# Hybrid decoder block on one core: attention scores in two PSUM tiles of 512 keys in place of one of 1024, the bias of the exponentials on ScalarE, and the sums without copies

## The chip, the core and the metric

The kernel runs on one core of one Trainium2 chip. The metric is the device time of one execution in microseconds (us). Before the change three runs gave 2529.47, 2530.45 and 2536.47 us, median 2530.45 us. One execution was profiled; it took 2535.77 us, with a span of 2534.0 us from its first to its last instruction.

Engines are named as the profile names them: PE (TensorE, matmuls), PEld (its weight loads), DVE (VectorE), ACT (ScalarE), POOL (GpSimd), SP (SyncE, which issues most DMAs). Each engine works through its own queue in order; what stands behind a waiting instruction waits too.

## The reference

One decoder sub-layer on x of 2048 tokens by 1024 channels: RMS norm, one input projection into seven parts, a gated linear recurrence (RG-LRU) in one branch, differential attention in the other, gates, an output projection and a second RMS norm. The change touches the attention:

```python
def diff_attention(q, k, v, lam):          # q, k: (B, S, 8 heads, 2 components, 64); v: (B, S, 8, 128)
    scale = HEAD_DIM ** -0.5
    outs = []
    for qb in range(S // Q_BLOCK):         # 16 blocks of 128 queries
        q0 = qb * Q_BLOCK; q1 = q0 + Q_BLOCK
        s = jnp.einsum('bqhcd,bkhcd->bhcqk', q[:, q0:q1], k[:, :q1]).astype(jnp.float32) * scale
        mask = (q0 + jnp.arange(Q_BLOCK))[:, None] >= jnp.arange(q1)[None, :]
        s = jnp.where(mask, s, -jnp.inf)
        p = jax.nn.softmax(s, axis=-1)
        w = p[:, :, 0] - lam * p[:, :, 1]
        outs.append(jnp.einsum('bhqk,bkhe->bqhe', w, v[:, :q1]))
    return jnp.concatenate(outs, axis=1)
```

Each head has two score matrices (components). Each gets a causal softmax of its own, the second is subtracted with the weight lam, and the difference multiplies v.

## The kernel before

The program has three stages. The first normalises x and runs the recurrence branch. The second, attention, also computes the projections q, k, v, za and gm as "fills" between its pieces of work. The third merges the branches. Every float32 matmul is done as three float16 matmuls (high by high, high by low, low by high).

Attention works in 128 units: 8 heads (h) of 16 query blocks (t), in this order. A unit has t+1 key blocks of 128 keys. They are cut into pieces of at most 8 blocks (1024 keys): one piece for t below 8, two from t = 8 on. The steps of a unit are:

- `a_scores(u, pi)` for one piece: the matmuls of line L804 write a PSUM tile `sc` of 128 queries x 2 components x 1024 keys, that is four PSUM banks. The pool `ps_s` has one such buffer, so the first matmul of a piece waits until DVE has read the whole piece before it. For each group of 512 keys there are six matmuls, three for each component; the components lie on rows 0 to 63 and 64 to 127 of the array. Then DVE copies each component into an SBUF tile `e` and takes the row maximum into a column of `mx` on the way (L819); the last 128 keys get the mask added (L823).
- `a_exp(u)`: DVE reduces the columns of `mx` to `rm` (L834) and makes the bias `nb` = -scale * maximum + a small term `lsp` (L837, a tensor_scalar with two per-partition scalars). ACT takes the exponentials of each component and piece in place, with their row sums into `sm` (L843).
- `a_comb(u)`, one unit later: DVE adds the sums of two pieces (L854), takes the reciprocal (L858), copies the sum of component 0 into `s0` for later (L859), makes the factor `rs` (L860) and combines the two components (L866). ACT rounds the result to float16 (L868), POOL makes the rest (L869), and SP issues DMA transposes into `pt` (L872).
- `a_pv(u)`, three units later (LAG = 3): matmuls of `pt` with V into the PSUM tile `o` (L889). After every fourth unit `a_norm` normalises four blocks and sends them to DRAM.

A fill is a group of matmuls into the PSUM tile `mm`: 24 of 512 columns for k, q or gm (L192), 48 of 256 columns for v and za (L696), followed by evictions on ACT and DVE. Which fill comes where is set by two things: the loop at the end of the stage counts how many fills are due per unit (the string ORD gives the order of steps in a unit), and the framework that builds the program then orders each engine's queue with a cost model of its own, by what it takes to be ready, so rows of different steps interleave. [...]

Of the kernel before, what the change touches and what calls it, by code (L numbers as in the profile page):

```python
# [9 lines left out]
F32 = mybir.dt.float32  # L10
# [4 lines left out]
AF = mybir.ActivationFunctionType  # L15
# [9 lines left out]
CH = 512  # L25
# [23 lines left out]
def kernel(  # L49
# [44 lines left out]
    with ExitStack():  # L94
# [485 lines left out]
        with ExitStack() as ax:  # L580
# [11 lines left out]
            ps_s = ax.enter_context(tc.tile_pool(name="ps_s", bufs=1, space=PSUM))  # L592
# [192 lines left out]
            def a_scores(u, pi):  # L785

                h, t = u.h, u.t
                if pi == 0:
                    u.n = 1 if t == 0 else (2 if t <= 8 else 3)
                    u.mx = t4.tile([128, 2, 3], F32, tag="mx", name="mx")  # L790
                    u.e = {}
# [3 lines left out]
                pss = ps_s.tile([128, 2, 1024], F32, tag="sc", name="sc")  # L795
                q0 = (t % 4) * 128
                Q = Qt[h, t // 4]
                for x in range(0, nb, 4):
                    m = min(4, nb - x) * 128
                    K = Kt[h, (b0 + x) // 4]  # L800
                    for i, (a, b) in enumerate(((0, 0), (0, 1), (1, 0))):
                        for ci in range(2):
                            r = slice(64 * ci, 64 * ci + 64)
                            nc.tensor.matmul(pss[:, ci, x * 128:x * 128 + m], Q[r, a, q0:q0 + 128], K[r, b, 0:m],  # L804
                                             start=(i == 0), stop=(i == 2))
                last = b0 + nb == t + 1
                m = (nb - 1 if last else nb) * 128
                for ci in range(2):
                    ps = pss[:, ci]
# [7 lines left out]
                    col = pi  # L817
                    if m:
                        nc.vector.tensor_scalar(out=ev[:, 0:m], in0=ps[:, 0:m], scalar1=1.0, scalar2=None,  # L819
                                                op0=ALU.mult, op1=ALU.max, accum_out=u.mx[:, ci, col:col + 1])  # L820
                        col += 1
                    if last:
                        nc.vector.tensor_tensor_reduce(out=ev[:, m:m + 128], in0=ps[:, m:m + 128], in1=mask,  # L823
                                                       op0=ALU.add, op1=ALU.max, scale=1.0, scalar=-3e38,
                                                       accum_out=u.mx[:, ci, col:col + 1])
# [20 lines left out]
            def a_comb(u):  # L846
                h, t = u.h, u.t
                pcs = pieces(t)
                if t % 4 == 0:
                    s0_t[h, t // 4] = t4.tile([128, 4], F32, tag="s0", name="s0")  # L850
# [350 lines left out]
```

## Time and profile before

| | before |
|---|---|
| median of 3 runs | 2530.45 us (2529.47 to 2536.47) |
| profiled execution, time / span | 2535.77 us / 2534.0 us |
| attention stage in that span (first score matmul to last product with V) | about 480 to 1986 us |
| mean granted TensorE clock | 0.976 |
| PE busy, share of the span | 2338.9 us, 92% |
| DVE busy | 1549.1 us, 61% |
| ACT busy | 1224.8 us, 48% |
| POOL busy | 672.9 us, 27% |

The profile's page lists, for each group of instructions, the busy time, the mean length of one in ns, and the idle time of the engine just before them with what ended it. A window row gives, for a stretch of the span, the busy time of PE, PEld, DVE, ACT and POOL (the number of instructions in brackets), then the granted PE clock, the share of DMA and GB/s. A row of the timeline gives start, length, engine, line, operation, output and inputs, count, and in square brackets the engine's idle time before it. "PE sc L804 <- DVE e L819" in the view of waits reads: PE, at the matmuls of line 804 into `sc`, waited for the instruction of line 819 on DVE.

### The profile page before, as it was taken

The page shows a single profiled execution, that of the slowest core. Times are in us where ns is not written, and L with a number is a line of the kernel's source. Part 1 is how long each engine was busy: PE and PEld are TensorE (multiplying, and loading weights), DVE is VectorE, ACT ScalarE, POOL GpSimd, SP SyncE. Part 2 cuts the span into 40 slices and gives each one's busy share as a digit, 9 for nine tenths or more (in the row PEclk, how much of TensorE's full clock was granted, in tenths as well). Part 3 has the DMA queues.
Part 4 walks back from the last instruction along what each step waited for, and adds up shares of the span by engine and source line. Part 5 has one row for each costly group of instructions (what it writes and reads, how often), then busy time and mean ns, then how long its engine had stood idle before and what let it go on. Part 6 is the DMA issues. An engine that isn't in the chain of part 4 may idle for free. (4 is left out here: it accounts for less than half of the span.)

```text
span 2534.0 us, 42086 instructions
## 1 busy us (share of the span) xinstructions
PE 2338.9 (92%) x15880; PEld 1303.1 (51%) x15880; DVE 1549.1 (61%) x4316; ACT 1224.8 (48%) x2156; POOL 672.9 (27%) x415
## 2 busy tenths in 40 slices
PE   5699999898997999998998998898999799999998
PEld 5344444455654555654654654555655344444443
DVE  7877767667667567568568466467567244634323
ACT  5455545556556456556556455456455244312211
POOL 2343334222213213222123122222223133322211
PEclk9899999999999999999999999999999899999999
DMA  9511111134434435436335335334334844743202
GB/s 242 103 42 45 47 42 34 50 81 96 92 69 99 95 62 113 81 59 125 73 64 127 56 77 109 70 74 114 68 73 103 261 156 135 227 163 110 90 17 100
DMA packets 511627, 243.58 MB, mean 96 GB/s; under 512 B 365384, under 2 KB 488320, under 8 KB 511424
## 3 DMA queue, kind: packets, MB, share of 16 engines
q1 hardware_dynamic: 508448, 231.56, 38.0%
q0 software_dynamic: 2816, 9.08, 1.2%
q8 instruction: 124, 2.03, 0.3%
q14 instruction: 79, 0.65, 0.1%
q10 hardware_dynamic: 160, 0.27, 0.0%
HBM read 110.79 MB, written 41.94 MB: 60 GB/s over the span
## 5 line engine op out<-in xcount | busy, mean ns | idle before, releaser
L192 PEld LDWEIGHTS <-w 128*128 128x128 f16 x5040 | 473.6, 100 | 618.7 <-issue 132.2
L192 PE MATMUL mm<-uT,w 128*128 128x512 f16 x3072 | 707.2, 388 | 25.3 <-ACT gm L713 16.4
L869 POOL TENSOR_TENSOR e<-e,e 128x1024 f16<-128x1024 f32 (+2 forms) x192 | 310.9, 1633 | 859.4 <-ACT e L868 421.5
L843 ACT ACTIVATE e<-e,nb,sc_h 128x1024 f32<-128x1024 f32 (+7 forms) x384 | 376.3, 981 | 209.3 <-DVE nb L837 142.8
L192 PE MATMUL ps<-uT,w 128*128 128x512 f16 (+1 forms) x1968 | 351.0, 343 | 31.6 <-ACT xr L318 20.7
L696 PE MATMUL mm<-wva,uT 128*128 128x256 f16 x3072 | 350.2, 274 | 3.8 <-DVE wva L178 2.5
L1086 PE MATMUL psb<-yt,w 128*128 128x512 f16 x1536 | 336.2, 382 | 4.9 <-DMA yt<-ya_d 3.4
L819 DVE TENSOR_SCALAR_CACHE_REDUCE e<-sc 128x1024 f32<-128x1024 f32 (+7 forms) x352 | 304.8, 879 | 37.1 <-PE sc L804 32.0
L696 PEld LDWEIGHTS <-uT 128*128 128x128 f16 x3072 | 297.0, 98 | 56.8 <-issue 19.9
L804 PE MATMUL sc<-K,Q 64*128 64x512 f16 (+3 forms) x1920 | 214.6, 351 | 49.7 <-DVE e L819 34.5
L1086 PEld LDWEIGHTS <-w 128*128 128x128 f16 x1536 | 149.7, 98 | 187.7 <-issue 8.2
L889 PE MATMUL o<-V,pt 128*128 128x128 f16 x3264 | 215.9, 220 | 28.3 <-DMA pt<-e 28.2
L889 PEld LDWEIGHTS <-pt 128*128 128x128 f16 x3264 | 189.4, 98 | 73.5 <-DMA pt<-e 34.8
L868 ACT ACTIVATE e<-e 128x1024 f16<-128x1024 f32 (+2 forms) x192 | 150.1, 802 | 138.3 <-DVE e L866 135.4
L866 DVE SCALAR_TENSOR_TENSOR e<-e,rs,e 128x1024 f32<-128x1024 f32 (+2 forms) x192 | 194.7, 1041 | 2.6
L804 PEld LDWEIGHTS <-Q 64*128 64x128 f16 x1920 | 78.1, 95 | 153.8 <-DVE e L819 40.1
L1117 PE MATMUL psf<-wo,m 128*128 128x512 f16 x720 | 155.7, 379 | 0.0
L156 ACT ACTIVATE jk<-wst 128x1024 bf16<-128x1024 f32 x80 | 84.3, 1053 | 140.4 <-DMA wst<-in_w_in_dram 103.2
L1117 PEld LDWEIGHTS <-m 128*128 128x128 f16 x768 | 75.1, 98 | 90.6
L1090 DVE SCALAR_TENSOR_TENSOR t<-gt,psb 128x512 f32<-128x512 f32 x64 | 43.9, 686 | 120.7 <-PE psb L1086 100.1
L916 POOL TENSOR_TENSOR y<-y,y 128x512 f16<-128x512 f32 x32 | 43.4, 1357 | 261.2 <-ACT y L913 238.7
L854 DVE TENSOR_TENSOR s<-sm 128x2 f32<-128x2 f32 x64 | 11.7, 182 | 155.9 <-ACT e L843 155.8
(249 smaller groups left out, 2398.0 us busy)
## 6 DMA issues: line engine op xcount, KB each, us to landing
wst<-in_w_in_dram SPq DMA_DIRECT2D x64, 512.0 KB, 4.4
xt<-in_x_dram SPq DMA_DIRECT2D x32, 512.0 KB, 4.5
gm_d<-gm SPq DMA_DIRECT2D x64, 256.0 KB, 2.6
gt<-gm_d SPq DMA_DIRECT2D x32, 512.0 KB, 3.8
ya_d<-yT SPq DMA_DIRECT2D x64, 128.0 KB, 2.0
wst<-in_w_br_rnn_dram SPq DMA_DIRECT2D x16, 512.0 KB, 4.5
wst<-in_w_br_attn_dram SPq DMA_DIRECT2D x16, 512.0 KB, 4.5
wost<-in_w_out_dram SPq DMA_DIRECT2D x16, 512.0 KB, 3.6
```

What stands on the lines that cost most here:

```text
L156: nc.scalar.activation(jk, w.st, AF.Square, accum_out=ss)
L192: nc.tensor.matmul(ps, w.t[:, a, k, :], uT[:, b, k, c0:c0 + n], start=(i == 0), stop=(i == 3 * KD - 1))
L696: nc.tensor.matmul(ps[:, j, :], uT[:, a, k, s0:s0 + 128], wt[:, b, k].rearrange("p t f -> p (t f)"), start=(i == 0), stop=(i == 3 * KD - 1))
L804: nc.tensor.matmul(pss[:, ci, x * 128:x * 128 + m], Q[r, a, q0:q0 + 128], K[r, b, 0:m], start=(i == 0), stop=(i == 2))
L819: nc.vector.tensor_scalar(out=ev[:, 0:m], in0=ps[:, 0:m], scalar1=1.0, scalar2=None, op0=ALU.mult, op1=ALU.max, accum_out=u.mx[:, ci, col: ...
L843: nc.scalar.activation(ev[:, 0:nb * 128], ev[:, 0:nb * 128], AF.Exp, bias=nb_[:, ci:ci + 1], scale=sc_h[h], accum_out=u.sm[:, pi, ci:ci + 1])
L866: nc.vector.scalar_tensor_tensor(out=e0[:, 0:m], in0=e1v[:, 0:m], scalar=rs, in1=e0[:, 0:m], op0=ALU.mult, op1=ALU.add)
L868: nc.scalar.activation(e1[:, 0, 0:m], e0[:, 0:m], AF.Copy)
L869: nc.gpsimd.tensor_tensor(out=e1[:, 1, 0:m], in0=e0[:, 0:m], in1=e1[:, 0, 0:m], op=ALU.subtract)
L889: nc.tensor.matmul(o, pt[:, a, kb % 8, :], V[:, kb % 4, b, :], start=(kb == 0 and i == 0), stop=(kb == n - 1 and i == 2))
L1086: nc.tensor.matmul(ps, w.t[:, p, k, :], y_t[b][:, q, k, sl], start=(i == 0), stop=(i == 3 * KD - 1))
L1117: nc.tensor.matmul(pn[n], m16[:, a, j, ms], wo[:, b, j, ns], start=(j == 0 and a == 0 and b == 0), stop=(j == KD - 1 and a == 1))
```

## The change

The score tile becomes 128 x 2 x 512 (two banks), and the pool has two of them; a piece of 1024 keys uses both, one after the other. DVE copies each tile of 512 keys out by itself, each with its own column of `mx` (up to five columns instead of three). The `e` tiles in SBUF, the exponentials and all that follows keep their sizes of up to 1024 keys. The bias `nb` is made on ACT by an activation with scale and bias given per partition. The sums of the exponentials of a unit with one piece are accumulated directly into the tile `s0`, and the sum over two pieces is written there; the copy of L859 is gone.

```diff
-            ps_s = ax.enter_context(tc.tile_pool(name="ps_s", bufs=1, space=PSUM))
+            ps_s = ax.enter_context(tc.tile_pool(name="ps_s", bufs=2, space=PSUM))
...
                 if pi == 0:
-                    u.n = 1 if t == 0 else (2 if t <= 8 else 3)
-                    u.mx = t4.tile([128, 2, 3], F32, tag="mx", name="mx")
+                    u.n = t // 4 + (2 if t % 4 else 1)
+                    u.mx = t4.tile([128, 2, 5], F32, tag="mx", name="mx")
...
-                pss = ps_s.tile([128, 2, 1024], F32, tag="sc", name="sc")
...
-                for x in range(0, nb, 4):
-                    m = min(4, nb - x) * 128
-                    K = Kt[h, (b0 + x) // 4]
-                    for i, (a, b) in enumerate(((0, 0), (0, 1), (1, 0))):
-                        for ci in range(2):
-                            r = slice(64 * ci, 64 * ci + 64)
-                            nc.tensor.matmul(pss[:, ci, x * 128:x * 128 + m], Q[r, a, q0:q0 + 128], K[r, b, 0:m],
-                                             start=(i == 0), stop=(i == 2))
-                last = b0 + nb == t + 1
-                m = (nb - 1 if last else nb) * 128
...
-                    if m:
-                        nc.vector.tensor_scalar(out=ev[:, 0:m], in0=ps[:, 0:m], scalar1=1.0, scalar2=None,
-                                                op0=ALU.mult, op1=ALU.max, accum_out=u.mx[:, ci, col:col + 1])
-                        col += 1
-                    if last:
-                        nc.vector.tensor_tensor_reduce(out=ev[:, m:m + 128], in0=ps[:, m:m + 128], in1=mask,
-                                                       op0=ALU.add, op1=ALU.max, scale=1.0, scalar=-3e38,
-                                                       accum_out=u.mx[:, ci, col:col + 1])
+                for x in range(0, nb, 4):
+                    w = min(4, nb - x)
+                    K = Kt[h, (b0 + x) // 4]
+                    ps = ps_s.tile([128, 2, CH], F32, tag="sc", name="sc")
+                    for i, (a, b) in enumerate(((0, 0), (0, 1), (1, 0))):
+                        for ci in range(2):
+                            r = slice(64 * ci, 64 * ci + 64)
+                            nc.tensor.matmul(ps[:, ci, 0:w * 128], Q[r, a, q0:q0 + 128], K[r, b, 0:w * 128],
+                                             start=(i == 0), stop=(i == 2))
+                    last = b0 + x + w == t + 1
+                    m = (w - 1 if last else w) * 128
+                    col = (b0 + x) // 4
+                    for ci in range(2):
+                        ev = u.e[ci, pi][1][:, x * 128:(x + w) * 128]
+                        if m:
+                            nc.vector.tensor_scalar(out=ev[:, 0:m], in0=ps[:, ci, 0:m], scalar1=1.0, scalar2=None,
+                                                    op0=ALU.mult, op1=ALU.max, accum_out=u.mx[:, ci, col:col + 1])
+                        if last:
+                            k = col + 1 if m else col
+                            nc.vector.tensor_tensor_reduce(out=ev[:, m:m + 128], in0=ps[:, ci, m:m + 128], in1=mask,
+                                                           op0=ALU.add, op1=ALU.max, scale=1.0, scalar=-3e38,
+                                                           accum_out=u.mx[:, ci, k:k + 1])
...
-                nc.vector.tensor_scalar(out=nb_, in0=rm, scalar1=nsc_h[h], scalar2=lsp, op0=ALU.mult, op1=ALU.add)
-                u.sm = t4.tile([128, 2, 2], F32, tag="sm", name="sm")
+                nc.scalar.activation(nb_, rm, AF.Identity, scale=nsc_h[h], bias=lsp)
+                if t % 4 == 0:
+                    s0_t[h, t // 4] = t4.tile([128, 4, 2], F32, tag="s0", name="s0")
+                u.s = s0_t[h, t // 4][:, t % 4, :]
+                if t >= 8:
+                    u.sm = t4.tile([128, 2, 2], F32, tag="sm", name="sm")
...
-                                             scale=sc_h[h], accum_out=u.sm[:, pi, ci:ci + 1])
+                                             scale=sc_h[h], accum_out=(u.sm[:, pi, ci:ci + 1] if t >= 8 else u.s[:, ci:ci + 1]))
...
-                nc.vector.tensor_copy(out=s0, in_=s[:, 0:1])
```

The queues are ordered anew, since the framework sees other tiles. Two places show what the prediction speaks of.

The first is DVE at the unit h = 1, t = 14 (after its first tile is scored). Before, with `e_8166` and `e_8168` the SBUF tiles of its first piece, `y` the output of `a_norm`, `wva` the weights of v and za, `e_7914`, `e_8003` the tiles of the unit before:

```order
L910 SCALAR_TENSOR_TENSOR y<-o,rv,G 128x128 x4
L854 TENSOR_TENSOR s<-sm 128x2
L858 RECIPROCAL rs<-s 128x1
L859 COPY s_7971<-s 128x1
L860 SCALAR_TENSOR_TENSOR rs<-s,nlam,rs 128x1
L866 SCALAR_TENSOR_TENSOR e_7914<-e_7916,rs,e_7914 128x1024
L866 SCALAR_TENSOR_TENSOR e_8003<-e_8006,rs,e_8003 128x768
L178 SCALAR_TENSOR_TENSOR wva<-wst,w_sg_aza,wva 128x8x128
L819 TENSOR_SCALAR e_8166,mx<-sc 128x1024
L819 TENSOR_SCALAR e_8168,mx<-sc 128x1024
```

And now, with `e_8171` and `e_8172` the same two tiles (lines of the changed kernel: L820 is the copy out, L856 the sum, L865 the combination):

```order
L178 SCALAR_TENSOR_TENSOR wva<-wst,w_sg_aza,wva 128x8x128
L164 TENSOR_SCALAR w_tot<-tot 128x1
L105 TENSOR_SCALAR pb<-w_tot 128x1
L107 TENSOR_SCALAR w_sg_agm<-pb 128x1
L820 TENSOR_SCALAR e_8171,mx<-sc 128x512
L115 TENSOR_SCALAR w_iv_agm<-w_sg_agm 128x1
L820 TENSOR_SCALAR e_8172,mx<-sc 128x512
L171 SCALAR_TENSOR_TENSOR w_cz<-w_iv_agm,cu 128x1
L820 TENSOR_SCALAR e_8171,mx<-sc 128x512
L820 TENSOR_SCALAR e_8172,mx<-sc 128x512
L856 TENSOR_TENSOR s_7879<-sm 128x2
```

Two copies out have become four of half the size, and they stand ahead of the sums and the combinations of the unit before instead of behind them; the copy L859 is gone.

The second is PE at the first piece of h = 4, t = 15, where its first 512 keys end (`sc` with a number is one PSUM tile, `pt` and `o` belong to the product with V). Before:

```order
L804 LDWEIGHTS Q_14548
L804 MATMUL sc_15266<-K_12966,Q_14548 128x512
L804 LDWEIGHTS Q_14548
L804 MATMUL sc_15266<-K_13612,Q_14548 128x512
L804 LDWEIGHTS Q_14548
```

And now:

```order
L812 LDWEIGHTS Q_14598
L812 MATMUL sc_15326<-K_13015,Q_14598 128x512
L888 LDWEIGHTS pt_14983
L888 MATMUL o_15425<-V_13139,pt_14983 128x128
L812 LDWEIGHTS Q_14598
L812 MATMUL sc_15335<-K_13653,Q_14598 128x512
```

The two halves of a piece go to different tiles, and other matmuls may stand between them. Over the whole queue the score matmuls form 194 unbroken runs before and 245 now; their number, 1920, and that of all other matmuls is the same.

On ACT each unit's exponentials now have an activation of 128 x 2 for `nb` ahead of them in the queue (128 more instructions).

More of the change, by code (lines that the diff above doesn't have):

```diff
@@ L794, in a_scores @@
                 b0, nb = pieces(t)[pi]
-                pss = ps_s.tile([128, 2, 1024], F32, tag="sc", name="sc")
                 q0 = (t % 4) * 128
                 Q = Qt[h, t // 4]
-                for x in range(0, nb, 4):
-                    m = min(4, nb - x) * 128
-                    K = Kt[h, (b0 + x) // 4]
-                    for i, (a, b) in enumerate(((0, 0), (0, 1), (1, 0))):
-                        for ci in range(2):
-                            r = slice(64 * ci, 64 * ci + 64)
-                            nc.tensor.matmul(pss[:, ci, x * 128:x * 128 + m], Q[r, a, q0:q0 + 128], K[r, b, 0:m],
-                                             start=(i == 0), stop=(i == 2))
-                last = b0 + nb == t + 1
-                m = (nb - 1 if last else nb) * 128
                 for ci in range(2):
-                    ps = pss[:, ci]
                     if ci == 0:
@@ L816, in a_scores @@
                     u.e[ci, pi] = (e, ev)
-                    col = pi
-                    if m:
-                        nc.vector.tensor_scalar(out=ev[:, 0:m], in0=ps[:, 0:m], scalar1=1.0, scalar2=None,
-                                                op0=ALU.mult, op1=ALU.max, accum_out=u.mx[:, ci, col:col + 1])
-                        col += 1
-                    if last:
-                        nc.vector.tensor_tensor_reduce(out=ev[:, m:m + 128], in0=ps[:, m:m + 128], in1=mask,
-                                                       op0=ALU.add, op1=ALU.max, scale=1.0, scalar=-3e38,
-                                                       accum_out=u.mx[:, ci, col:col + 1])
+                for x in range(0, nb, 4):
[20 more added lines that the diff above has]
+                                                           accum_out=u.mx[:, ci, k:k + 1])
             s0_t = {}
@@ L848, in a_comb @@
                 pcs = pieces(t)
-                if t % 4 == 0:
-                    s0_t[h, t // 4] = t4.tile([128, 4], F32, tag="s0", name="s0")
-                s0 = s0_t[h, t // 4][:, t % 4:t % 4 + 1]
+                s = u.s
                 if len(pcs) == 2:
-                    s = t4.tile([128, 2], F32, tag="s", name="s")
                     nc.vector.tensor_tensor(out=s, in0=u.sm[:, 0], in1=u.sm[:, 1], op=ALU.add)
-                else:
-                    s = u.sm[:, 0]
                 rs = t4.tile([128, 1], F32, tag="rs", name="rs")
                 nc.vector.reciprocal(out=rs, in_=s[:, 1:2])
-                nc.vector.tensor_copy(out=s0, in_=s[:, 0:1])
                 nc.vector.scalar_tensor_tensor(out=rs, in0=s[:, 0:1], scalar=nlam, in1=rs, op0=ALU.mult, op1=ALU.mult)
@@ L902, in a_norm @@
                 v = t4.tile([128, 4], F32, tag="v", name="v")
-                nc.vector.tensor_scalar(out=v, in0=s0, scalar1=kap_h[h], scalar2=None, op0=ALU.mult)
+                nc.vector.tensor_scalar(out=v, in0=s0[:, :, 0], scalar1=kap_h[h], scalar2=None, op0=ALU.mult)
                 nc.vector.tensor_tensor(out=v, in0=v, in1=v, op=ALU.mult)
```

## The prediction

> **What bounds the kernel now.** I read the page first, then the attention stage alone, then what PE waits for there.
>
> ```profile
> PE 2338.9 (92%) x15880; PEld 1303.1 (51%) x15880; DVE 1549.1 (61%) x4316; ACT 1224.8 (48%) x2156; POOL 672.9 (27%) x415
> 480.00:1990.00 1510.00, 1399.04 (x11206) 844.96 (x11205) 981.82 (x3232) 833.77 (x1695) 360.30 (x228) 0.98 0.41 88
> ```
>
> The first row is the page's, the second the window of the attention stage. PE is busy for 1399.04 of 1510.00 us there and idle for 111; DVE is busy for 65% and ACT for 55%. PE is the bound, and since the change leaves its matmuls as they are, what it can win lies in those 111 us. The view of waits tells what ended them:
>
> ```profile
> PE sc L804 <- DVE e L819: 34.5, 19, 10.0
> PE o L889 <- DMA pt<-e: 28.2, 22, 3.0
> PE sc L804 <- DVE mx L823: 7.9, 12, 1.1
> PE sc L804 <- DVE rs_a L124: 2.2, 1, 2.2
> PE sc L804 <- DVE w_tot L164: 2.0, 1, 2.0
> PE sc L804 <- DVE w_iv_agm L115: 1.6, 1, 1.6
> ```
>
> The columns are the total in us, the number of waits and the longest. 48 us are score matmuls that wait for the one score tile to be read out. The next row, 28.2 us, is products with V that wait for the transposes. The change works on the first kind.
>
> **The score tile in halves: the waits.** PE may write the first 512 keys of a piece as soon as the first 512 keys of the piece before are read, instead of all 1024. What that is worth is the time between the two:
>
> ```profile
> 1007.62 1.22 DVE L819 TENSOR_SCALAR_CACHE_REDUCE e<-sc 128x1024 f32<-128x1024 f32 x1
> 1008.76 0.08 DVE L819 DVE_READ_ACCUMULATOR e<-sc 128x1 f32 x1
> 1347.90 0.68 DVE L819 TENSOR_SCALAR_CACHE_REDUCE e<-sc 128x512 f32<-128x512 f32 x1
> 1348.51 0.08 DVE L819 DVE_READ_ACCUMULATOR e<-sc 128x1 f32 x1
> ```
>
> These timeline rows give what an eviction takes until DVE's next instruction can start: 1.14 us for 1024 keys (1008.76 - 1007.62), 0.61 us for 512 (1348.51 - 1347.90). A whole piece of two components takes 2.28 us, its first half 1.22 us, so a wait can shrink by 1.06 us, not more, as long as DVE begins as late as before. Of the 34.5 us, one wait has 10.0; the other 18 have 24.5, a mean of 1.36. Their ceiling is 18 x 1.06 = 19 us; since several must be shorter than 1.06 us I take 15. The twelve of the mask row are at most 1.1 us each, so all 7.9 us go. The three single ones give 3 x 1.06 = 3.2 us. Together 26.1 us; the bounds are 0 and 48.
>
> The 10 us wait is a case of its own:
>
> ```profile
> 813.03 1.12 DVE L910 SCALAR_TENSOR_TENSOR y<-o,rv,G 128x128 f32<-128x128 f32 x4 [3.52 <-DMA gm_d<-gm]
> 814.08 0.15 DVE L854 TENSOR_TENSOR s<-sm 128x2 f32<-128x2 f32 x1
> 817.75 3.14 DVE L178 SCALAR_TENSOR_TENSOR wva<-wst,w_sg_aza,wva 128x1024 f16<-128x1024 f32 x1
> 820.80 1.21 DVE L819 TENSOR_SCALAR_CACHE_REDUCE e<-sc 128x1024 f32<-128x1024 f32 x1
> 823.23 2.42 PE L804 MATMUL sc<-K,Q 64*128 64x512 f16 x12 [9.99 <-DVE e L819]
> 825.63 6.45 PE L192 MATMUL mm<-uT,w 128*128 128x512 f16 x24
> 833.41 5.35 PE L192 MATMUL mm<-uT,w 128*128 128x512 f16 x24
> 813.20:835.00 21.80, 11.81 (x58) 4.60 (x58) 14.42 (x33) 11.57 (x19) 6.36 (x3) 0.77 0.50 122
> ```
>
> The evictions at 820.80 stood behind the sums and combinations (814.08 to 817.75, 3.67 us). This is the first place that the change's order shows, and there they come ahead of these. So this wait loses 3.67 + 1.06 = 4.7 us; nothing to 10 are its bounds. Behind it PE ran slow: the same 24 matmuls took 6.45 us instead of 5.35, the score matmuls 2.42 us, and the granted clock was 0.77 in that window. That is some 2 us: 1.1 from the 24 and about 1 from the scores. Whether PE still runs slow behind a wait of 5 us is open, so I take 1 of the 2. [...]
>
> **The score tile in halves: what it costs PE.** A run of score matmuls has a price of its own where it begins or ends:
>
> ```profile
> 962.89 0.82 PE L804 MATMUL sc<-K,Q 64*128 64x512 f16 x6 [0.58 <-DVE s L859]
> 963.64 5.41 PE L696 MATMUL mm<-wva,uT 128*128 128x256 f16 x48
> 968.99 1.47 PE L804 MATMUL sc<-K,Q 64*128 64x512 f16 x12
> 970.39 0.18 PE L162 MATMUL tot<-w_s,ones 128*128 128x1 bf16 x1
> ```
>
> Six matmuls take 0.75 us to the next start (963.64 - 962.89), twelve take 1.40 (970.39 - 968.99), and twice six would be 1.50: 0.10 us for a split. The order has 245 runs in place of 194, so 51 x 0.10 = 5.1 us are added to PE, and nothing hides them.
>
> **What it costs and frees on DVE.** The forms of L819 and the instructions that go:
>
> ```profile
> L819 DVE TENSOR_SCALAR_CACHE_REDUCE e<-sc 128x1024 f32<-128x1024 f32 x128 | 151.4, 1219 | 14.5 <-PE sc L804 12.0 <-DMA pt<-e 2.4
> L819 DVE TENSOR_SCALAR_CACHE_REDUCE e<-sc 128x896 f32<-128x896 f32 x32 | 34.7, 1086 | 3.5 <-PE sc L804 2.4 <-POOL e L869 1.1
> L819 DVE TENSOR_SCALAR_CACHE_REDUCE e<-sc 128x768 f32<-128x768 f32 x32 | 30.4, 951 | 2.0 <-PE sc L804 2.0
> L819 DVE TENSOR_SCALAR_CACHE_REDUCE e<-sc 128x640 f32<-128x640 f32 x32 | 26.2, 818 | 3.2 <-PE sc L804 3.2
> L837 DVE TENSOR_SCALAR nb<-rm,nsc_h,lsp 128x2 f32<-128x2 f32 x120 | 49.0, 409 | 2.5
> L859 DVE COPY s<-sm 128x1 f32<-128x1 f32 x64 | 9.7, 152 | 41.8 <-ACT e L843 41.8
> L859 DVE COPY s<-s 128x1 f32<-128x1 f32 x64 | 8.6, 135 | 0.0
> ```
>
> The four forms above 512 keys, 128 + 3 x 32 = 224 instructions, are split in two. Each split costs 2 x 0.61 - 1.14 = 0.08 us, 17.9 us in all. The 120 biases (49.0 us) and the 128 copies (18.3 us) go. DVE is some 49 us freer in the stage. I count nothing for that: DVE is idle for 528 us of it, and what matters is when an eviction starts, which is priced above. Were this slack gone, it would be a further gain.
>
> **The bias on ACT.** The trace has no activation of this shape. Near it stand the exponentials, which also take scale and bias per partition:
>
> ```profile
> L843 ACT ACTIVATE e<-e,nb,sc_h 128x256 f32<-128x256 f32 x32 | 18.8, 587 | 5.9 <-DVE nb L837 5.9
> L843 ACT ACTIVATE e<-e,nb,sc_h 128x128 f32<-128x128 f32 x32 | 15.4, 481 | 5.7 <-DVE nb L837 5.7
> 1017.73 0.29 DVE L837 TENSOR_SCALAR nb<-rm,nsc_h,lsp 128x2 f32<-128x2 f32 x1
> 1018.12 1.24 ACT L843 ACTIVATE e<-e,nb,sc_h 128x1024 f32<-128x1024 f32 x1 [0.19 <-DVE nb L837]
> ```
>
> From 256 columns to 128 an exponential gets 106 ns shorter, so at 2 columns it would be 481 - 106 = 375 ns; 128 of them are 48 us more on ACT, 58% busy then instead of 55%. On the way from the maxima to the exponentials the old bias took 0.39 us (1018.12 - 1017.73) and the new one 0.375 plus the way from DVE to ACT, which the old one paid too: 0.1 us later, or earlier where DVE was slow (its 409 ns are a mean, the row above shows 0.29 us). What that delays is the transposes, so the 22 waits of `o` on `pt`: 22 x 0.1 = 2.2 us. The bounds are 0 and 48 us, every bias in full on PE.
>
> **The end of the stage.** After the last scores PE has too little to do until the last products:
>
> ```profile
> 1973.91 1.44 PE L889 MATMUL o<-V,pt 128*128 128x128 f16 x19 [2.26 <-DMA pt<-e]
> 1980.23 0.28 PE L889 MATMUL o<-V,pt 128*128 128x128 f16 x2 [0.39 <-DMA pt<-e]
> 1983.50 2.74 PE L889 MATMUL o<-V,pt 128*128 128x128 f16 x46 [2.99 <-DMA pt<-e]
> ```
>
> Three waits of 5.6 us. In the new order 47 fill matmuls and 126 of the products stand between the last scores and the first product of the last unit, where 45 and 45 stood. The additional 81 products take 2.74 / 46 = 0.06 us each, 4.8 us, and cover most of this; I take 4 us, between 0 and 5.6.
>
> **What comes back.** Where PE reaches a product sooner, but the transposes come no sooner, the wait shows there. 34 waits are cut in 128 units, about a quarter of the units; so a quarter of the 22 waits for `pt` may grow by 1.06 us, 6 us. The bounds are 0 and all that the waits give.
>
> **The sum.** -26.1 - 4.7 - 1 + 5.1 + 2.2 - 4 + 6 = -22.5 us. Against the profiled execution (2535.77 us, that is its span of 2534.0 and 1.8 around it) this is 2513.3. That execution is 5.3 us above the median, so on the scale of the median 2508. The ends of the costs give 2530 - 48 - 2 - 5.6 + 5.1 = 2480 and, with no gain and all of the bias, 2530 + 5 + 48 = 2583.
>
> **Rivals.** The waits stay (0.18). They are ended by DVE's queue: the evictions come late because sums, combinations and weights stand ahead of them, and four small ones behind the same work help only by the half piece. For it: three of the six rows of waits name instructions (rs_a, w_tot, w_iv_agm) that have nothing to do with scores. Against it: the place in the order where the evictions moved forward. Then some 15 us are gained, 8 lost to runs and the bias, and half of the rest comes back: 2526.
>
> The scores run ahead (0.09). With two tiles the framework puts scores earlier, and the waits for `pt` (28.2 us) go too, together with the 48: half of the 28.2 on top of the forecast with nothing coming back gives 2508 - 14 - 6 = 2488. Against it: each `e` tile is still held until its transposes are done, which limits how far scores can run ahead, and their number is unchanged.
>
> Slower (0.18). The bias in ACT's queue becomes the pace. It stands behind whatever ACT does then, and DVE waits for the exponentials before it can go on to evictions:
>
> ```profile
> DVE s L854 <- ACT e L843: 155.8, 54, 5.1
> ```
>
> Each of these waits grows by the bias, and behind the waiting sum stand the next evictions. If all 128 biases came through in full, 48 us would meet the gain: 2508 + 48 - 2 = 2554. It decides from about 24 us, 63 of the biases, on. For it: 54 of the 64 sums wait already. Against it: ACT is idle for 45% of the stage, and PE waits for transposes only 22 times in 128 units. [...]
>
> **Chances.** The forecast, a gain of 10 to 40 us, has 0.55; the four make 1. About 0.3%, 7.6 us, is what a measurement can tell from no change. Faster: the forecast and the scores that run ahead, 0.64. Same: the waits stay, 0.18. Slower: 0.18. The range of 8 in 10 goes from 2480, the lower end of the sum, to 2542, where half of the slower rival's cost is in. The forecast's own range is 2490 to 2521.
>
> **What would show it.** The waits of scores for DVE at 15 to 22 us instead of 48; no score wait of 10 us; score runs of six at 0.75 us to the next start; the copies out at 576 and their 512-key form near 683 ns; an ACT activation of 128 x 2 at 0.3 to 0.4 us; PE idle in the stage at 80 to 90 us; waits for `pt` near 30 us. If score waits fall by 25 us and the span does not, something that came back is larger than 6 us. If DVE's wait for the exponentials grows by over 20 us and score waits with it, the slower rival is right.

## The result: 2518.5 us instead of 2531.1, with the forecast at 2508

The changed kernel takes 2518.49 us, median of 7 runs (2514.63 to 2521.97), the kernel before beside it 2531.11 us (7 runs, 2529.47 to 2536.47). The ratio is 0.9946 with an interval of 0.9936 to 0.9956, so 11 to 16 us faster. The forecast had 22.5. Direction and range held; the main reason given for them, as will be seen, did not.

The first row of the changed kernel's page:

```profile
PE 2341.8 (93%) x15880; PEld 1298.0 (52%) x15880; DVE 1509.0 (60%) x4508; ACT 1267.7 (50%) x2284; POOL 664.1 (26%) x415
```

The window of its attention stage:

```profile
480.00:1990.00 1510.00, 1415.71 (x11263) 844.49 (x11261) 944.55 (x3432) 882.28 (x1834) 351.70 (x229) 0.99 0.42 90
```

The span is 2519.8 us instead of 2534.0. It is PE's busy time plus PE's idle time, and this sum is the frame for all that follows: busy went from 2338.9 to 2341.8 (+2.9), idle from 195.1 to 178.0 (-17.1). In the window of the stage PE is idle for 94.3 us (1510.00 - 1415.71), where it was 111. The merge stage's first PE instruction of weight (`tot<-ya_t`) starts at 1998.63 us instead of 2012.79, so the attention stage holds the whole difference.

What PE waits for in that window now (total us, number, longest):

```profile
PE sc L812 <- DVE e L820: 28.2, 26, 2.3
PE mm L192 <- ACT gm L713: 19.5, 7, 4.0
PE sc L812 <- DVE mx L824: 6.7, 6, 2.3
PE mm L696 <- DVE w_tot L164: 5.9, 5, 2.5
PE tot L162 <- DVE w_s L158: 5.2, 4, 2.0
PE mm L696 <- DVE Q L667: 4.8, 5, 1.4
PE o L888 <- DMA pt<-e: 4.6, 6, 1.1
PE tot L162 <- ACT gm L713: 4.4, 1, 4.4
...
PE sc L812 <- DVE rs L858: 1.2, 1, 1.2
```

Two things differ from what was announced. The score waits, which were to fall from 48 to 15-22 us, are at 36 (28.2 + 6.7 + 1.2). The waits of products for `pt`, which were to stay near 30, are at 4.6. And small waits of fills grew: for `w_tot`, `Q` and a `gm` of 4.4 us.

The same change seen from DVE, its waits over the whole span:

```profile
DVE s L856 <- ACT e L848: 108.9, 42, 5.6
...
DVE rs L858 <- ACT e L848: 73.4, 46, 3.6
...
DVE e L820 <- DMA pt<-e: 34.2, 16, 3.7
```

And two of the groups by shape:

```profile
L820 DVE TENSOR_SCALAR_CACHE_REDUCE e<-sc 128x512 f32<-128x512 f32 x384 | 249.4, 686 | 71.3 <-DMA pt<-e 34.2 <-PE sc L812 32.4 <-POOL e L868 4.3
...
L838 ACT ACTIVATE nb<-rm,lsp,nsc_h 128x2 f32<-128x2 f32 x120 | 46.2, 385 | 151.3 <-DVE rm L835 151.2
```

The copies out wait 34.2 us for `e` tiles that the transposes still read; before it was 2.6 (and 2.9 for the copies with the mask). The bias costs ACT 385 ns (the estimate was 375).

One place in the changed kernel shows what the half tiles do and do not do (PE and DVE rows of its timeline):

```profile
1143.70 0.82 PE L812 MATMUL sc<-K,Q 64*128 64x512 f16 x6
...
1144.57 0.82 PE L812 MATMUL sc<-K,Q 64*128 64x512 f16 x6
1144.61 0.16 DVE L856 TENSOR_TENSOR s<-sm 128x2 f32<-128x2 f32 x1 [2.50 <-ACT e L848]
...
1145.26 1.95 DVE L865 SCALAR_TENSOR_TENSOR e<-e,rs,e 128x1024 f32<-128x1024 f32 x2
...
1148.03 0.68 DVE L820 TENSOR_SCALAR_CACHE_REDUCE e<-sc 128x512 f32<-128x512 f32 x1
...
1148.64 0.69 DVE L820 TENSOR_SCALAR_CACHE_REDUCE e<-sc 128x512 f32<-128x512 f32 x1
...
1149.38 0.23 PE L812 MATMUL sc<-K,Q 64*128 64x128 f16 x2 [2.33 <-DVE e L820]
```

Both halves were written by 1145.4. DVE came to the first only at 1148.03: it had waited 2.50 us for the exponentials of the unit before, and then had its sums and combinations and some other small work to do. Once DVE had begun, the half tile worked as priced: PE went on after two copies of 512 keys and not after four. The wait is still 2.33 us, because the beginning was late.

### The profile page after: what moved, and what is told of

Same layout as the page of the kernel before. It is cut to its first block, busy times and chain, and to the rows that moved or that the text cites. A ratio compares the mean times of both kernels' runs of the same rounds, so it can differ in the third digit from the quotient of the medians.

```text
span 2519.8 us, 42351 instructions
## 1 busy us (share of the span) xinstructions
PE 2341.8 (93%) x15880; PEld 1298.0 (52%) x15880; DVE 1509.0 (60%) x4508; ACT 1267.7 (50%) x2284; POOL 664.1 (26%) x415
## 5 line engine op out<-in xcount | busy, mean ns | idle before, releaser
L868 POOL TENSOR_TENSOR e<-e,e 128x1024 f16<-128x1024 f32 (+2 forms) x192 | 302.7, 1591 | 893.3 <-issue 446.0
L820 DVE TENSOR_SCALAR_CACHE_REDUCE e<-sc 128x512 f32<-128x512 f32 (+3 forms) x576 | 327.3, 597 | 79.9 <-PE sc L812 40.1
L812 PE MATMUL sc<-K,Q 64*128 64x512 f16 (+3 forms) x1920 | 222.0, 347 | 37.7 <-DVE e L820 28.2
L865 DVE SCALAR_TENSOR_TENSOR e<-e,rs,e 128x1024 f32<-128x1024 f32 (+2 forms) x192 | 185.8, 995 | 2.7
L838 ACT ACTIVATE nb<-rm,lsp,nsc_h 128x2 f32<-128x2 f32 x120 | 46.2, 385 | 151.3 <-DVE rm L835 151.2
L915 POOL TENSOR_TENSOR y<-y,y 128x512 f16<-128x512 f32 x32 | 41.8, 1306 | 230.1 <-ACT y L912 219.8
```

The costliest lines, as they stand in the source:

```text
L812: nc.tensor.matmul(ps[:, ci, 0:w * 128], Q[r, a, q0:q0 + 128], K[r, b, 0:w * 128], start=(i == 0), stop=(i == 2))
L820: nc.vector.tensor_scalar(out=ev[:, 0:m], in0=ps[:, ci, 0:m], scalar1=1.0, scalar2=None, op0=ALU.mult, op1=ALU.max, accum_out=u.mx[:, ci, ...
L865: nc.vector.scalar_tensor_tensor(out=e0[:, 0:m], in0=e1v[:, 0:m], scalar=rs, in1=e0[:, 0:m], op0=ALU.mult, op1=ALU.add)
L868: nc.gpsimd.tensor_tensor(out=e1[:, 1, 0:m], in0=e0[:, 0:m], in1=e1[:, 0, 0:m], op=ALU.subtract)
```

## The experiments

Theory A is the prediction's: releasing the score tile in halves is what gains. Theory B: what gains is work taken from DVE (bias and copies). Theory C: only the new order of the queues, by chance. Twelve kernels were run in three groups. This table has each one's median, its ratio to the kernel before run beside it, and how its profiled span is made up. PE's busy time is the first number of the page's first row; idle is the span less that. The profiled execution is one of the runs and lies up to 6 us from the median, so the last three columns are read among themselves.

| kernel | median us | ratio (95%) | span | PE busy | PE idle |
|---|---|---|---|---|---|
| before | 2531.11 | 1 | 2534.0 | 2338.9 | 195.1 |
| changed | 2518.49 | 0.9946 (0.9936-0.9956) | 2519.8 | 2341.8 | 178.0 |
| split_only | 2555.82 | 1.0094 (1.0078-1.0109) | 2553.4 | 2356.7 | 196.7 |
| bias_only | 2515.79 | 0.9931 (0.9918-0.9943) | 2515.4 | 2336.9 | 178.5 |
| sums_only | 2525.94 | 0.9970 (0.9958-0.9982) | 2519.9 | 2334.8 | 185.1 |
| split_sums | 2536.45 | 1.0009 (1.0001-1.0018) | 2536.1 | 2353.5 | 182.6 |
| bias_sums | 2517.80 | 0.9944 (0.9924-0.9964) | 2514.9 | 2331.2 | 183.7 |
| evict_only | 2540.84 | 1.0033 (1.0019-1.0048) | 2542.7 | 2343.8 | 198.9 |
| bias_twice | 2543.71 | 1.0044 (1.0028-1.0059) | 2542.6 | 2346.2 | 196.4 |
| acc7 | 2537.16 | 1.0017 (1.0004-1.0030) | 2534.6 | 2335.7 | 198.9 |
| comb_after_bs | 2521.43 | 0.9957 (0.9944-0.9971) | 2519.2 | 2338.2 | 181.0 |
| comb_after_all | 2537.89 | 1.0024 (1.0012-1.0035) | 2529.7 | 2350.5 | 179.2 |
| after_acc7 | 2537.57 | 1.0024 (1.0014-1.0034) | 2533.3 | 2354.8 | 178.5 |
| evict_halves | 2761.43 | 1.0901 (1.0883-1.0919) | 2762.0 | 2430.8 | 331.2 |

None of these kernels leaves computation out. Where two experiments are set against each other, the number is the ratio of their ratios, which has no interval of its own.

### The parts one by one

**split_only**: the kernel before with the scores in two tiles of 512 keys and nothing else.

```diff
-            ps_s = ax.enter_context(tc.tile_pool(name="ps_s", bufs=1, space=PSUM))
+            ps_s = ax.enter_context(tc.tile_pool(name="ps_s", bufs=2, space=PSUM))
...
+                    ps = ps_s.tile([128, 2, CH], F32, tag="sc", name="sc")
...
+                        ev = u.e[ci, pi][1][:, x * 128:(x + w) * 128]
```

> The kernel before with the scores alone in two tiles of 512 keys; bias on DVE and copies of the sums as before. Theory A (the score tile, released in halves, is what gains): 2515 to 2522 us, 9 to 16 below the kernel before, with waits of the products for pt near 5 us as in the changed kernel (28 before) and score waits of 35 to 40 us (50 before). Theory B (the relief of DVE through bias and copies is what gains): within 4 us of the kernel before, waits for pt still 20 us or more. Theory C (only the new order of the queues moved the time, by chance): any value within 12 us of before, with no relation to the sum of the parts.

It is slower, by 0.94% or some 24 us. All three theories missed it, C with its 12 us as well. PE's row of the page:

```profile
PE 2356.7 (92%) x15880; PEld 1304.8 (51%) x15880; DVE 1568.3 (61%) x4764; ACT 1223.7 (48%) x2156; POOL 670.9 (26%) x415
```

Two of its waits in the stage up to 2000 us:

```profile
PE sc L812 <- DVE e L820: 55.4, 42, 5.4
...
PE o L890 <- DMA pt<-e: 1.9, 2, 1.0
```

The group of the score matmuls, and behind it the same group of the kernel before:

```profile
L812 PE MATMUL sc<-K,Q 64*128 64x512 f16 (+3 forms) x1920 | 229.0, 353 | 68.4 <-DVE e L820 55.4 <-DVE mx L824 6.4 <-ACT Q L666 4.9
```

```profile
L804 PE MATMUL sc<-K,Q 64*128 64x512 f16 (+3 forms) x1920 | 214.6, 351 | 49.7 <-DVE e L819 34.5 <-DVE mx L823 7.9 <-DVE rs_a L124 2.2
```

The waits of the score matmuls grew, 49.7 to 68.4 us, and those for `pt` vanished, 28.2 to 1.9. PE's idle time as a whole hardly moved (195.1 to 196.7). The loss is in PE's busy time, 17.8 us more for the same matmuls; the score group alone has 14.4 of it. What makes them longer is taken up under "Runs" and "The slow clock" below.

**bias_only**: the kernel before with the bias on ACT.

```diff
-                nc.vector.tensor_scalar(out=nb_, in0=rm, scalar1=nsc_h[h], scalar2=lsp, op0=ALU.mult, op1=ALU.add)
+                nc.scalar.activation(nb_, rm, AF.Identity, scale=nsc_h[h], bias=lsp)
```

> The kernel before with the bias of the exponentials on ACT alone. Theory A: within 4 us of before (2527 to 2535): DVE 49 us less busy, ACT 48 us more, both off the path. Theory B: 8 us or more below before, with waits for pt at half or less of 28 us. Theory C: anywhere within 12 us.

Faster by 0.69%, 17 us: this one line is worth as much as the whole change. The waits of PE in the stage:

```profile
PE o L889 <- DMA pt<-e: 28.9, 17, 4.7
PE sc L804 <- DVE e L819: 20.3, 15, 3.5
PE sc L804 <- DVE mx L823: 14.3, 11, 2.4
PE sc L804 <- DVE w_tot L164: 3.6, 1, 3.6
```

With the score tile still whole, the score waits are 38 us (20.3 + 14.3 + 3.6), nearly as low as in the changed kernel, and the wait of 10 us is gone. PE's idle time fell by 16.6 us. The time is what theory B said; its sign for `pt` did not come, these waits stayed at 28.9 us.

**sums_only**: the kernel before with the sums accumulated in place and no copies of line 859.

```diff
-                nc.vector.tensor_copy(out=s0, in_=s[:, 0:1])
...
-                nc.vector.tensor_scalar(out=v, in0=s0, scalar1=kap_h[h], scalar2=None, op0=ALU.mult)
+                nc.vector.tensor_scalar(out=v, in0=s0[:, :, 0], scalar1=kap_h[h], scalar2=None, op0=ALU.mult)
```

> The kernel before with the sums accumulated in place, without the 128 copies. Theory A: within 3 us of before, DVE 18 us less busy. Theory B: 3 to 5 us below before. Theory C: anywhere within 12 us.

Faster by 0.30%, some 8 us, more than theory B's 3 to 5. The gain is not in the score waits, whose largest row grew, and the long wait is still there (longest 9.9):

```profile
PE sc L804 <- DVE e L819: 40.2, 23, 9.9
```

**split_sums**: the changed kernel with the bias back on DVE.

```diff
-                nc.scalar.activation(nb_, rm, AF.Identity, scale=nsc_h[h], bias=lsp)
+                nc.vector.tensor_scalar(out=nb_, in0=rm, scalar1=nsc_h[h], scalar2=lsp, op0=ALU.mult, op1=ALU.add)
```

> The changed kernel with the bias still on DVE. Theory A: as split_only within 4 us, 2514 to 2522. Theory B: half of the gain or less, 2524 or more. Theory C: not between split_only and the changed kernel.

Within 0.2% of the kernel before. From here to the changed kernel the bias is worth 0.63% (0.9946 / 1.0009), 16 to 18 us. Theory A falls: half tiles alone lose, and without the bias on ACT the change gains nothing. Theory B's number held, and theory C's sign (not between split_only and the changed kernel) did not come.

### Is it DVE's time, and what does the split cost?

Theory D, from the first group: a microsecond of work on DVE around the evictions is worth about 0.37 us of time. Theory E: the gains come from the order, which every edit moves.

**bias_sums**: sums_only and bias_only together, so the changed kernel without the split.

> The kernel before with the bias on the activation engine and the sums without copies, scores still in one tile of 1024 keys. Theory D (what DVE does between an eviction and the next sets PE's waits; a microsecond taken from DVE there is worth about 0.37 us, from the 18 us that 49 us of biases gave): the two gains add, -18 and -8, so about 2505 to 2512 us, below the whole change. Theory E (the gains come from the order of the instructions, which every edit moves, and not from DVE's time): anything between 2510 and 2530, the gains need not add.

0.9944, some 14 us faster: neither better than bias_only nor worse than the whole change (0.9946). The gains of bias and sums do not add, against theory D. And the split brought nothing on top of them that can be measured.

```profile
PE 2331.2 (93%) x15880; PEld 1303.8 (52%) x15880; DVE 1497.3 (60%) x4060; ACT 1267.6 (50%) x2284; POOL 665.6 (26%) x415
```

Against this row the changed kernel has PE busy for 10.6 us longer (2341.8 - 2331.2) and idle for 5.7 us less.

**evict_only**: the kernel before, its one tile read out in pieces of 512 keys.

```diff
-                    if m:
-                        nc.vector.tensor_scalar(out=ev[:, 0:m], in0=ps[:, 0:m], scalar1=1.0, scalar2=None,
+                    for x in range(0, m, 512):
+                        y = min(x + 512, m)
+                        nc.vector.tensor_scalar(out=ev[:, x:y], in0=ps[:, x:y], scalar1=1.0, scalar2=None,
```

> The kernel before, with the evictions over 512 keys made in two instructions and nothing else: one score tile of 1024 keys, released as a whole. 17.9 us more on DVE. Theory D: 0.37 x 17.9 = 7 us slower, 2536 to 2541 us, so a third of what the split alone cost (22 us); the rest is then the half tiles' order and their 58 more score runs. If DVE's extra time were the whole price of the split it would be 22 us slower, 2553. Theory E: within 4 us of the kernel before, since the order of PE moves little (194 score runs as before).

Slower by 0.33%, some 8 us, where theory D had 7. If the longer eviction costs the same in split_only, it is about a third of the 24 us there; no run shows that. The score waits did not grow with the longer evictions, they fell to 27.5 us, and the waits moved to `pt`:

```profile
PE o L890 <- DMA pt<-e: 47.8, 21, 8.8
PE sc L804 <- DVE mx L824: 12.6, 13, 3.3
PE sc L804 <- DVE e L820: 9.6, 10, 4.3
```

**bias_twice**: the bias made twice on DVE, once into a tile that nobody reads.

```diff
+                nbx = t4.tile([128, 2], F32, tag="nbx", name="nbx")
+                nc.vector.tensor_scalar(out=nbx, in0=rm, scalar1=nsc_h[h], scalar2=lsp, op0=ALU.mult, op1=ALU.add)
                 nc.vector.tensor_scalar(out=nb_, in0=rm, scalar1=nsc_h[h], scalar2=lsp, op0=ALU.mult, op1=ALU.add)
```

> The kernel before with the bias computed twice on DVE, the first time into a tile that nobody reads: 49 us more on DVE, nothing else added. Theory D: the mirror of the bias on the activation engine, 15 to 20 us slower, 2546 to 2552 us, with score waits for DVE up from 50 to about 65 us. Theory E: the order of PE is close to that of the kernel with the bias on the activation engine (195 score runs, 193 runs of products with V, in both), so a gain like its 18 us should show here too, 2510 to 2525.

Slower by 0.44%, 11 us: the right side for theory D, less than its 15 to 20. DVE's busy time rose by 28 us (1549.1 to 1577.3), not by 49. Theory D's sign, score waits near 65 us, did not come; they stayed at 49:

```profile
PE sc L804 <- DVE e L819: 24.2, 11, 4.6
PE sc L804 <- DVE mx L823: 20.2, 13, 5.3
```

PE's idle time rose by 1.3 us alone, its busy time by 7.3. The granted clock over the span is 0.971 instead of 0.976, and PE works 109.0 us at half the clock instead of 92.5 (see "The slow clock" below), which is some 8 us. So more work on DVE goes with a longer time, but not by the waits that theory D named. Theory E's test does not decide either: in the profile this kernel has 194 score runs and 186 runs of products with V, which is nearer to the kernel before (194 and 183) than to bias_only (195 and 193).

**acc7**: the kernel before, fills spaced otherwise, the same instructions.

```diff
-ACC0 = 8.0
+ACC0 = 7.0
```

> The kernel before with the constant that spaces the fill matmuls (ACC0) at 7.0 in place of 8.0: the same instructions in another order, 190 runs of products with V in place of 183 and the fills elsewhere. A measure of what the order alone moves. Theory D: DVE's work is the same, so within 5 us of the kernel before. Theory E: 8 to 25 us off, to either side.

Slower by 0.17%, some 4 us. That is how far one other order moves the kernel with a whole tile, and effects below it are not to be read. One order more is a small sample.

### Why the score waits did not go

In each timeline I followed DVE back from every score wait above 0.1 us to the last point where DVE itself had been idle for over 0.25 us, and noted what ended that idle time. Of 49.6 us of score waits in the kernel before, 28.0 go back to a DVE that waited for ACT's exponentials (and the long wait of 10.0 to a DVE that waited for a DMA, the 3.52 us in the prediction's rows); of 68.3 in split_only 36.5; of 38.0 in bias_sums 28.3. Of 37.5 in the changed kernel it is 17.5, and 10.4 go back to `e` tiles that the transposes still read. Theory F: this wait, with an eviction behind it, is the cause. Theory G: the eviction's own length is.

**comb_after_bs**: bias_sums, and a small DVE instruction per unit that adds zero times the next unit's maxima to the sums. With it all 127 combinations stand behind the first eviction of the next unit. In bias_sums 78 stood ahead of it, by the first combination of each unit in DVE's order in the profile; the expectation has 87.

```diff
+                if nx is not None:
+                    sa = t4.tile([128, 2], F32, tag="sa", name="sa")
+                    nc.vector.scalar_tensor_tensor(out=sa, in0=nx.mx[:, :, 0], scalar=0.0, in1=s1,
+                                                   op0=ALU.mult, op1=ALU.add)
+                    s1 = sa
```

> One tile, bias on the activation engine, sums without copies, and one more small DVE instruction for each unit that ties its sums to the maxima of the next unit's first piece: all 127 combinations now stand behind the first evictions of the next unit, where 87 stood ahead of them. Some 26 us more on DVE, no work left out. Theory F (scores wait because DVE, in order, waits for the exponentials with an eviction behind it): score waits for DVE fall from 37 us to under 20, DVE's late evictions go, 2503 to 2512 us, unless products with V then wait for transposes by as much (30 us now, up to 45). Theory G (scores wait for the eviction's own length, whatever stands ahead): score waits stay at 33 to 42 us and the time rises by DVE's 26 us at 0.3, to 2522 to 2528.

It took 2521.43 us, 0.13% more than bias_sums (0.9957 / 0.9944). DVE's waits in bias_sums:

```profile
DVE s L855 <- ACT e L847: 158.2, 50, 5.6
DVE rs L857 <- ACT e L847: 75.9, 43, 2.9
...
DVE e L819 <- DMA pt<-e: 8.5, 5, 3.0
```

The same in this kernel:

```profile
DVE e L819 <- DMA pt<-e: 30.8, 25, 2.9
DVE s L861 <- ACT e L847: 12.3, 10, 5.5
...
DVE sa L857 <- ACT e L847: 4.2, 6, 1.0
```

And what PE waits for in it:

```profile
PE o L895 <- DMA pt<-e: 33.8, 27, 2.6
PE sc L804 <- DVE mx L823: 20.9, 15, 5.1
PE sc L804 <- DVE e L819: 6.9, 7, 1.6
```

The edit did what it was meant to: DVE's wait for the exponentials fell from 234.1 us (158.2 + 75.9) to 16.5, and 0.3 us of the score waits go back to it. Score waits fell from 37 to 29 us, though, not to under 20, and the time lies between the two theories' ranges. In the place of the exponentials came the `e` tiles: 30.8 us of evictions wait for transposes that still read the tile, and 8.1 us of the score waits go back to that; most of the rest goes back to other work of ACT (K, `jo` and `jk`, 14.8 us together). So theory F names the first thing that holds the evictions back, and the next ones stand right behind it.

**comb_after_all**: the same tie in the changed kernel.

> The same tie in the changed kernel (two tiles of 512 keys). Theory F: with nothing ahead of the evictions the half tiles can at last be refilled early; score waits from 38 to under 20 us, 2503 to 2514 us. Theory G: 38 stays, 2522 to 2530. Either way the score matmuls' busy time stays near 222 us, since the order has 240 runs of them against 245.

2537.89 us, slower than the changed kernel by 0.78% (1.0024 / 0.9946). The time is above the ranges of both theories. Score waits stay at 38 us (37.7 in the changed kernel), and the wait for `e` tiles is the largest of all the runs:

```profile
DVE e L820 <- DMA pt<-e: 57.8, 34, 3.4
```

Theory F fails for the half tiles: with nothing of the old unit ahead of the evictions, they wait for the transposes. 14.3 us of the score waits go back to that, 8.9 still to the exponentials.

### Orders

**after_acc7**: the changed kernel with the edit of acc7.

> The changed kernel with the constant that spaces the fills at 7.0 in place of 8.0: the same instructions in another order. If the half tiles are worth nothing and orders scatter by some 5 us, 2513 to 2525; if the order on record happened to be a bad one, below 2510.

2537.57 us, 0.78% or 19 us more than the changed kernel, with the same instructions. The upper end of what was expected is exceeded by 12.6 us. PE's row:

```profile
PE 2354.8 (93%) x15880; PEld 1304.6 (51%) x15880; DVE 1512.7 (60%) x4508; ACT 1267.1 (50%) x2284; POOL 663.3 (26%) x415
```

Its idle time is that of the changed kernel (178.5 to 178.0); all of the difference in the profiles, 13.0 us, is PE's busy time. The granted clock over the span is 0.974 instead of 0.979, and the order has 777 unbroken runs of matmuls into one kind of tile instead of 754 (200 runs of products with V instead of 185). The clock is enough for the difference: PE works 106.8 us at half the clock instead of 76.3, which is some 15 us (an estimate, see "The slow clock" below).

**evict_halves**: half pieces, but one whole tile. The words of the expectation call it the changed kernel; the file that ran has bias and copies as before, so it is split_only with the whole tile, and is set beside that. The framework now spreads the halves: 297 score runs (252 in split_only), of which 279 have six matmuls.

```diff
-            ps_s = ax.enter_context(tc.tile_pool(name="ps_s", bufs=2, space=PSUM))
+            ps_s = ax.enter_context(tc.tile_pool(name="ps_s", bufs=1, space=PSUM))
...
+                pss = ps_s.tile([128, 2, 1024], F32, tag="sc", name="sc")
...
-                    ps = ps_s.tile([128, 2, CH], F32, tag="sc", name="sc")
+                    ps = pss[:, :, x * 128:x * 128 + CH]
```

> The changed kernel with one tile of 1024 keys again, but written and read in halves of 512, so the order of PE has 297 score runs. Against the kernel with bias and sums alone (195 runs, score matmuls busy for 218 us): at 0.10 us a run, as my sum had it, score matmuls are busy for 228 us and the time is about 2535 with the extra evictions; at 0.23 us (mean start to next start of six matmuls twice, less that of twelve) 241 us and about 2548.

9% slower than the kernel before and 8% slower than split_only (1.0901 / 1.0094), far from any number expected. PE's row of the page and two of its waits in the stage up to 2000 us:

```profile
PE 2430.8 (88%) x15880; PEld 1318.9 (48%) x15880; DVE 1576.3 (57%) x4764; ACT 1228.7 (44%) x2156; POOL 661.5 (24%) x415
```

```profile
PE o L891 <- DMA pt<-e: 99.2, 57, 8.6
PE sc L813 <- DVE e L821: 52.7, 30, 6.4
```

PE is idle for 331.2 us. In the order other matmuls stand between the halves of a piece, and the tile stays taken from the first to the last. How much of the 8% is the tile and how much the other order was not separated. The score matmuls are busy for 251.8 us, but at a granted clock of 0.937, so this number does not settle the price of a score run. One correction belongs here: the 0.23 us of the expectation was not worked out rightly. It was a mean over timeline rows of twelve matmuls, and such a row names only its first shape: rows that last 1.24 or 0.92 us to the next start hold a group of 384 or 128 keys. Where both groups have 512 keys it is 1.40 us for twelve and 0.75 for six, the prediction's 0.10 us. That is the way out of the scores alone; "Runs" below has the way in.

## Why the prediction was right, and where it was not

**The number** was right in sign, and the size was 56% of the forecast (12.6 of 22.5 us). By the frame of busy and idle: forecast busy +4 (+5.1 for runs, -1 for the slow clock), measured +2.9; forecast idle -26.6, measured -17.1. That the number lies in the range is luck: the largest term is not there, two others were too small by 5 and 7 us with opposite signs, and most of the gain comes from work that was counted at nothing.

**The half tiles, -26.1.** This is the step that failed. Score waits fell by 12.0 us (49.7 to 37.7), not 26, and bias_only gets nearly the same fall with a whole tile (to 39.5). The half piece of 1.06 us is there at the one place looked at, as the rows at 1149.38 show; the condition "as long as DVE begins as late as before" is what did not hold. Evictions wait for `e` tiles (34.2 us instead of 2.6), and scores that are allowed ahead by the order meet that wait. In four pairs that differ by the split (alone; over the sums; over sums and bias; over these and the tie), PE idle changed by +1.6, -2.5, -5.7 and -1.8 us: that is what the half tiles gave.

**The long wait, -4.7.** It is gone, but also in bias_only, which keeps the whole tile, and it stays in sums_only. The order moved evictions ahead of the sums in some places, not in most: of 127 combinations, 82 stood ahead of the next unit's first eviction before, and 62 do now (by DVE's order in the two profiles). I took one row of the order for the rule.

**Runs, +5.1.** This term counted half of what a run costs. The 0.10 us is lost where scores end and other matmuls begin. Where scores begin it is lost once more, as two fills of the kernel before show, each with the row behind it:

```profile
738.46 5.34 PE L192 MATMUL mm<-uT,w 128*128 128x512 f16 x24
743.73 1.47 PE L804 MATMUL sc<-K,Q 64*128 64x512 f16 x12
...
986.59 5.34 PE L192 MATMUL mm<-uT,w 128*128 128x512 f16 x24
991.76 0.50 PE L889 MATMUL o<-V,pt 128*128 128x128 f16 x6
```

The same 24 matmuls take 5.27 us to the start of scores and 5.17 us to the start of products. Over that whole trace, at the full clock, a fill matmul of 512 columns takes 216 ns to the start of another fill and also to that of a product, but 312 ns to that of a score; a score matmul of 512 keys takes 308 ns to the start of a fill or a product and 212 ns to that of the next group of keys. A product takes 56 ns to the start of another product and also to that of a fill. So a run costs 0.19 us, 51 runs 9.8 us, and a change between fills and products costs nothing. The rows give the score matmuls as `64*128` and the fills and products as `128*128`, so each run is two changes of shape; whether the shape is what costs the 0.10 us at each was not tested.

In the four pairs PE's busy time rose by 17.8, 18.7, 10.6 and 12.3 us, with 46 to 58 more score runs, which at 0.19 are 9 to 11. In the first two pairs most of the rest is the granted clock.

**The slow clock, -1.** In the clock records of all these traces the granted clock is either 1.0 or 0.5 (at 0.5 for 122.3 us of the span in the kernel before, for 104.6 in the changed one), and at 0.5 the same fill matmul takes 427 ns instead of 216. PE works 92.5 us at 0.5 in the kernel before and 76.3 in the changed one, and about half of such time is lost, so the clock as a whole gave some -8 us where this term had -1. If half of it is taken off, PE's busy time is 2289.4 to 2292.6 us in the eight kernels with a whole tile, 2301.4 to 2304.3 in the five with half tiles and 2316.9 in evict_halves. By this estimate the split costs PE 11 to 13 us in each of the four pairs, and the +2.9 us of the whole change are some +11 for the runs and -8 for the clock. Why the clock is low for longer in one kernel than in another was not tested.

**DVE's relief, counted at nothing.** The other half of the failed step. The bias on ACT is worth 17 us alone, 16 to 18 over the split, some 7 over the sums, and doubling it on DVE costs 11: four pairs, all on the same side. That an engine that is idle for a third of the time sets the pace, because what it does in order between two waits decides when the next eviction begins, fits the waits followed back above (28.0 of 49.6 us) and the idle time that bias_only saves. It is not shown to be the whole cause: every edit also moves the order, the score waits of bias_twice did not grow, and part of its loss is the clock. Breaking up the copies out alone was evict_only, and it lost 8 us.

**The bias, +2.2, and what comes back, +6.** The duration was right (385 against 375 ns). The waits for `pt` did not grow by 8 us; they fell by 23.6, as the rival "the scores run ahead" had it. The split does this (1.9 in split_only, 30.4 in bias_sums); that scores stand further ahead of the products in its order was not measured. But this gain was paid for: the waits of fills for DVE's small instructions and for ACT's `gm` (`mm` and `tot` together, over the whole span) rose from 56.9 to 74.7 us, a line that my sum did not have.

**The end of the stage, -4.** Right. Of three waits of 5.6 us one of 0.42 is left:

```profile
1967.35 2.74 PE L888 MATMUL o<-V,pt 128*128 128x128 f16 x46 [0.42 <-DMA pt<-e]
```

**The rival "the waits stay"** (0.18) came nearest in mechanism: 37.7 of 49.7 us of score waits are still there, and DVE's queue ends them, with sums and combinations of the unit before ahead of the evictions. Its time of 2526 us is 8 too long; it counted nothing for DVE's relief or for the clock.

**The slower rival** did not happen: DVE's waits for the exponentials are no longer than before (182.3 us in the two rows of the changed kernel, 155.8 + 41.8 + 26.2 = 223.8 before), with 43 us more on ACT.

What stays open: the worth of the split to better than some 15 us. Four pairs give +0.02% to +0.94%, never a gain, yet two orders of the changed kernel lie 19 us apart. Whether the changed kernel's order is a lucky one, or that of after_acc7 an unlucky one, two orders do not tell. For the same reason the 17 us of bias_only are not free of its order: one other order of the whole tile moved it by 4 us, one of the half tiles by 19. The smallest change with the full gain is bias_only.

## What to carry to other kernels

Before pricing a wait by the length of the instruction that ends it, follow the engine back to its own last idle time; if that is a wait for a third engine, shortening the instruction may win little (here the split changed PE's idle time by +1.6 to -5.7 us), and taking small work out of that engine's queue may win more (here the bias alone took 16.6 us off it). When a framework orders the queues, run one other order of the same instructions: the distance between the two is the least that an edit must bring before its reason can be believed. And split PE's time into busy and idle, since an edit that only touches waits can lose in the busy part (split_only lost 17.8 us there); then look how much of the busy part ran at the lower clock.

## What the hardware showed that was not expected

PE's busy time for the same 15880 matmuls ran from 2331.2 to 2356.7 us in the kernels with idle times of 178 to 199 us, with granted clocks of 0.971 to 0.979, and to 2430.8 us at a clock of 0.937 where PE was idle for 331.2. It is no constant to which waits are added. Two orders of the same instructions with the same idle time (178.0 and 178.5 us) differed by 13.0 us of it, and the granted clock differed in all their runs: 0.977 to 0.980 in the seven of the changed kernel, 0.971 to 0.976 in the twelve of after_acc7.
